# Strassen steps' first sums: transfers bound to leave one raw load sooner, four places for them instead of two, and steps of seven units in other places

## The chip, the cores and the metric

One core of one Trainium2 chip. The metric is the device time of one execution in microseconds. The kernel before took 2371.19 us, the median of three runs (2370.3 to 2372.21).

Names used below: PE is TensorE, DVE is VectorE, ACT is ScalarE, POOL is GpSimd, SP is SyncE. SP and POOL only issue DMA transfers here, apart from a few masks on POOL. Each engine works through its own list of instructions in order, so an instruction that waits holds up everything behind it on that engine.

## The reference

A decoder block on 256 tokens of width 4096, in float32:

```
h    = rmsnorm(x)
proj = h @ w_in                       # 4096 x 20480
u_p, z_p, u_c, b_c, c_c, z_c, g = split(proj)     # 6 x 2048, then 2 x 4096
y_pool = (causal pooling of u_p, then 4 maps 512x512) * pool_scale * silu(z_p)
y_conv = b_c * conv3(c_c * u_c) * silu(z_c)
br     = y_pool @ w_branch[0], y_conv @ w_branch[1]
merged = sum over both of sigmoid(g + gate_b) * br
out    = rmsnorm(x + merged @ w_out)
```

Nearly all arithmetic is the three products with w_in, w_branch and w_out. The inputs have 256 rows, so 128 partitions hold half of the tokens.

## The kernel before

**Units and steps.** The output columns are cut into 32 units of 1024 columns (the list `units`): twelve of the two mixers (cu0, cc0, cz0, cb0, cu1, cc1, cz1, cb1, pz0, pu0, pz1, pu1), eight gates (g0_0, g1_0, g0_1 ... g1_3), eight branch units (b0_0 ... b1_3) and four output units (o0 ... o3). A unit is a sum over 16 steps (8 in the branch units); a step multiplies 256 input channels, as stationary operands in the buffer `arena`, with one block of weights of 256 x 1024, which is 1 MB. The weights come once from memory, so each step needs one load of its block into one of three buffers of `raw` (NRAW = 3), issued by SP. The block is split into a high and a low part in fp32r (rounded by ACT, the rest subtracted by DVE), kept in a ring buffer (`ring`), and each product is three matmuls: high by high, high by low, low by high.

**P steps and S steps.** A plain step (P) makes 24 matmuls of 128x128 by 128x512; ACT and DVE make one pair of instructions for each half of the block. A Strassen step (S) makes 7 products instead of 8, so 21 matmuls, but its weights must be combined first. In `Step.micros` (kind "S") that is, on DVE: `sums` (V = first quarter of the block + two others), a subtraction for the three direct quarters, two additions into W, and one subtraction each for V's and W's low part; on ACT three roundings. S steps thus spare PE three matmuls and cost DVE several instructions. `PLACES` and `OUT` say which of a unit's 16 places hold S steps; for pz1 and g0_0 only how many there are counts, since `insert` weaves steps of the pooling branch ("B", "M") into these two units and orders the rest itself: P P B P M M P P, then the S steps in equal groups with one P between.

**Helped steps.** For the S steps that `HELPED` lists (by their number within the unit) the first sum need not be made on DVE. SP copies the first quarter of the block twice into a half of the buffer E (128 x 1024), POOL then adds the two other quarters to it with an accumulating DMA (`move_add`), and `sums` falls away; the load into `raw` leaves the first quarter out (768 KB). The two halves of E are the slots 0 and 1 (`place_of_sum`). `pump` sends such a transfer out when all of these hold:

- the step's unit is the running one, and E is free of the unit's epilogue: `e_done` writes into `sums_from` from which tick on (a tick is six matmuls);
- a slot is free (the step that had it has made its parts, `summed`);
- the step's own raw load is among the next ones: its number is below the number of the next load to be issued, `state["nl"]`, plus LEAD = 3, and not below `state["nl"]` + LATEST with LATEST = 0.

If the last bound is missed, the step is dropped from the list and makes its sum on DVE. "k loads ahead" below means that the step's own raw load is number `state["nl"]` + k when the copy is issued. The accumulating DMA is put on POOL's list WAIT = 1 raw load later.

**The order of the program.** Everything is laid out by a planner in Python when the kernel is built. `pump` issues raw loads as soon as the raw buffer's step is read, prepares steps up to AHEAD = 3 ahead of the running one as far as the ring has room, and issues the transfers of helped steps; `tick` runs one item of `queue`, the epilogue of the unit before (joining the Strassen sums into R, transposes on PE, gates, stores), and one item of the fills of `arena` for the branch units (`pop_fill`). E and R are the epilogue's buffers: banks are evacuated into E at a unit's end, R collects the unit's result. `joins` writes R once all S steps of the unit are done. `conv_units`, `pool_units`, `mix`, `gate_unit` and `out_unit` hold the epilogues with their stores of R (`z_d`, `gates_d`, `o_d`, by POOL).

Of the kernel before, what the change touches and what calls it, by code (L numbers as in the profile page):

```python
# [56 lines left out]
def hybrid_block(ctx: ExitStack, tc: tile.TileContext, x, x_t, norm_t, w_first, w_in, pool_w, pool_scale,  # L57
# [50 lines left out]
    R = sb("R", [P, 2, NU])  # L108
    E = sb("E", [P, 2, NU])
# [360 lines left out]
    def halves(fn):  # L470
        return [lambda t=t: fn(t) for t in range(2)]

    sums_from = [None]

    def e_done(n=2):

        def f():
            sums_from[0] = now[0] + n
        return f

    def combine(u):
# [67 lines left out]
    def gap(n):  # L549
        return [None] * n  # L550
# [66 lines left out]
    def at_places(at):  # L617
# [3 lines left out]

    few = NS_X - NB
    LAST_FIRST = ('cc0',)
    HELPED = {'cc0': (1, 2, 4, 5), 'cz0': (1, 2, 5), 'cb0': (1, 2, 4, 5, 7, 8), 'cu1': (1, 2, 4, 5, 7, 8), 'cc1': (1, 2, 4, 7, 8), 'cz1': (1, 2, 4, 5, 7), 'cb1': (1, 2, 4, 5, 7, 8), 'pz0': (1, 4, 5, 7), 'pu0': (1, 2, 4, 5, 7), 'pz1': (1, 2, 4, 5, 6, 7, 8), 'pu1': (1, 2, 4, 5, 7), 'g0_0': (1, 2, 4, 5, 7), 'g1_3': (1, 2, 5), 'g1_0': (1, 2, 4, 5, 8), 'g0_1': (1, 2, 4, 5, 6, 7), 'g1_1': (1, 4, 5, 7, 8), 'g0_2': (1, 2, 3, 4, 5, 7, 8), 'g1_2': (1, 2, 4, 5, 7, 8), 'g0_3': (1, 2, 4, 5, 7, 8), 'o0': (1, 2, 4, 5), 'o1': (1, 2, 4, 5, 7), 'o2': (1, 2, 4, 5), 'o3': (0, 2, 4, 5)}
    PLACES = {
# [19 lines left out]
    }  # L645
    GATE = (2, 4, 5, 7, 8, 10, 11, 13, 15)

# [149 lines left out]
    def mix(st):  # L797
        g = st.g
        for t in range(2):
            o = shared(2 * g + t)  # L800
            ts = slice(t * P, (t + 1) * P)
            for k in range(4):
                for i, (a, b) in enumerate(((st.ah, st.h), (st.ah, st.l), (st.al, st.h))):
                    pin(nc.tensor.matmul(o, a[:, k, ts], b[:, k], start=(k, i) == (0, 0), stop=(k, i) == (3, 2)))  # L804
        rg.release(st.bw, 16)
        rg.release(st.ba, 8)
        cs = slice(g * NH, (g + 1) * NH)
        for t in range(2):
            mul(R[:, t, cs], shared(2 * g + t), Y[:, t, cs])
        if g == 1:  # L810
            c = st.c

            def copy(j):
                act(chan(E)[:, 2 * j:2 * j + 2], bankview(j))
            queue.extend(gap(3) + transposes(R, copy) + [lambda: put(y_d[0, c], chan(E)), e_done(8)])


    def gate_unit(n, c, before=None):
# [214 lines left out]
    last = units[-1]  # L1033
# [175 lines left out]

    x_with = {0: (1, 2), 1: (2, 4), 3: (4, 6), 4: (6, 8), 5: (8, 10), 6: (10, 12)}  # L1210

    LATEST = 0
    LEAD, WAIT = 3, 1
    adding = deque()

    def pump():

        while True:
            moved = False
            nl = state["nl"]  # L1220
            if nl < len(loaded) and (nl < NRAW or loaded[nl - NRAW].split):
                issue_load(loaded[nl])
                state["nl"] += 1

                if nl in x_with:
                    load_x(*x_with[nl])
                moved = True
            while helped and (helped[0].prepared or helped[0].load_index < state["nl"] + LATEST):
                helped.pop(0)
            if helped and helped[0].host is running[0] and sums_from[0] is not None and now[0] >= sums_from[0] and (  # L1230
                    helped[0].load_index < state["nl"] + LEAD):
                t = helped[0]
                at = next((i for i in t.slots if sums_in[i] is None or sums_in[i].summed), None)
                if at is not None:
                    helped.pop(0)
                    t.slot, sums_in[at] = at, t
                    w, v = t.src.rearrange("p k n -> p (k n)"), place_of_sum(at)
                    load(v, w[:, None, 0:NH].to_broadcast([P, 2, NH]))
                    adding.append((state["nl"] + WAIT, t, v, w[:, NH:3 * NH]))
                    moved = True  # L1240
            while adding and (adding[0][0] <= state["nl"] or adding[0][1].load_index < state["nl"]):
                _, t, v, w = adding.popleft()
                move_add(v.rearrange("p i n -> p (i n)"), w)
                t.added = True
                moved = True
            i = state["np"]
            if i < len(steps) and i <= state["limit"]:
                s = steps[i]
                if s.src is None or s.raw is not None:
                    if state["micros"] is None:  # L1250
                        state["micros"] = deque(s.micros())
                    if state["micros"]:
                        size, guard, fn = state["micros"][0]
                        if guard is None or guard():
                            block = rg.alloc(size) if size else True
                            if block is not None:
                                state["micros"].popleft()
                                fn(block)
                                moved = True
                    if not state["micros"]:  # L1260
                        s.prepared = s.split = True
                        state["micros"] = None
                        state["np"] += 1
                        moved = True
            if not moved:
                return
# [5 lines left out]
    for u in units:  # L1272
        for k, s in enumerate(t for t in u.steps if t.kind == "S"):
            if k in HELPED.get(u.name, ()):
                helped.append(s)
        s_at = [i for i, t in enumerate(u.steps) if t.kind == "P"]
        for i, t in enumerate(u.steps):
            t.slots = (0, 1)[:1 + (i < s_at[-1])] if t.kind == "S" else ()
    sums_in = [None] * 2
    running = [None]  # L1280

    def tick():
# [91 lines left out]
    for u in units:  # L1374
        if u.name == "pu1":
            make_bands(1)
            u.steps[2].first.append(lambda: end_bands(1))
        if u is last_x:
            Y = replace_by("y_b", lower).tile([P, 2, NU], F32, name="Y")
            stages.append(replace_by("more").tile([P, 4, P], F32, name="sb"))  # L1380

            in_y = [Y.rearrange("p a n -> p (a n)")[:, i * 4 * P:(i + 1) * 4 * P].rearrange("p (k c) -> p k c", k=4) for i in range(2)]
            stages.extend(in_y)
        if u is last:
            break
        sums_from[0] = None
        if u is units[1]:
            e_done()()
        for st in u.steps:
            assert st.prepared, (u.name, st.kind)  # L1390
            if st is u.steps[0]:
                running[0] = u
            if st is u.steps[-1]:
                running[0] = None
                assert all(t is None or t.summed for t in sums_in)
            run_step(u, st)
            state["now"] += 1
            if u is last_x and st is u.steps[12]:
                units_done[0] = True
            if u.s and not u.flags.get("joined") and st is not u.steps[-1] and u.closed(*SHARED):  # L1400
                assert not queue, u.name
                queue.extend(joins(u))
            pump()
            if u is units[units.index(last_x) - 1] and st is u.steps[14]:
                queue_fills()
            if u.before and st is u.steps[len(u.steps) * 3 // 4]:
                assert not queue, u.name
                if u.name == "b0_0":
                    del stages[2:]
                    assert not any(f.st is q for f in fills for q in in_y)  # L1410
                u.before()
        while queue:
            f = queue.popleft()
            if f:
                f()
        combine(u)
        queue.extend(u.epi(u))
        state["mm"] = 0
        pump()

# [6 lines left out]
        parked[c] = raw[:, i % NRAW].rearrange("p (t n) -> p t n", t=2)  # L1427
        load(parked[c], o_d[c])

    sums_from[0], running[0] = None, last  # L1430
    lead = last.steps[:-TAIL]
    combined = False
    for st in lead:
# [153 lines left out]
```

## Time and profile before

| what | value |
|---|---|
| median of three runs | 2371.19 us |
| the profiled execution | 2372.17 us |
| its span in the profile | 2370.1 us |
| matmuls | 10474 |
| PE busy | 2351.0 us, 99% |
| DVE busy | 2187.4 us, 92% |
| ACT busy | 1422.8 us, 60% |
| moved by DMA | 590.92 MB, 249 GB/s |
| TensorE clock granted | 0.999 of full |

The profiled execution's time is 2.07 us above its span, what lies before the first and behind the last instruction. The profile lists groups of instructions by line and tile, waits (which engine stood idle, and what ended that), stretches of time with each engine's busy share, and each engine's instructions in order of time. The start of a unit is the start of its first matmul.

### The profile page before, as it was taken

The numbers are of one execution on the slowest core, as the hardware profiler recorded it, in microseconds if no ns is written. First come the engines' busy times: TensorE is split into PE (matmuls) and PEld (weight loads), VectorE is DVE, ScalarE is ACT, GpSimd is POOL, SyncE is SP. The second block draws the span as 40 slices with busy tenths as digits, with TensorE's granted clock in tenths as the row PEclk, the third lists the DMA queues.
The fourth block names the chain that finished last, engine by engine and source line by source line (L and its number), as shares of the span: only waits on it lengthen the run. The fifth ranks groups of instructions, "written<-read, shape, count | busy, mean of one in ns | idle before, by whom it ended". The sixth has DMA issues, their size and how long they took to land.

```text
span 2370.1 us, 28071 instructions
## 1 busy us (share of the span) xinstructions
PE 2351.0 (99%) x10474; PEld 1944.1 (82%) x10474; DVE 2187.4 (92%) x2247; ACT 1422.8 (60%) x1477; POOL 133.3 (6%) x200
## 2 busy tenths in 40 slices
PE   9999999999999999999999999999999999999998
PEld 7888888887888888888888888888788888888886
DVE  8999999989999989989989999998998898899898
ACT  7565665666556666566656656565664556566564
POOL 0000000000001001000000000001100001000000
PEclk9999999999999999999999999999999999999999
DMA  8576777766877657757887887788866667778767
GB/s 336 184 243 206 248 261 244 254 222 215 272 269 233 227 205 246 235 215 249 275 265 244 284 269 239 253 287 282 280 239 236 238 236 284 241 232 287 237 236 268
DMA packets 104841, 590.92 MB, mean 249 GB/s; under 512 B 11200, under 2 KB 11456, under 8 KB 50176
## 3 DMA queue, kind: packets, MB, share of 16 engines
q1 hardware_dynamic: 82944, 498.14, 57.5%
q0 software_dynamic: 21328, 89.93, 16.1%
q8 instruction: 82, 1.34, 0.2%
q10 hardware_dynamic: 432, 1.07, 0.1%
q14 instruction: 55, 0.45, 0.0%
HBM read 556.58 MB, written 25.17 MB: 245 GB/s over the span
## 4 chain that ended last, share of the span: by engine, by line
PE 89%; DVE 6%; DMA 3%; ACT 1%; issue 1%; DVEq 0%; SPq 0%; ACTq 0%
PE sums L1294 66%; PE shared L1294 21%; DVE ring L72 3%; DMA raw<-in_w_out_dram 1%; ACT ring L69 1%; DVE W L72 1%; PE shared L804 1%; PE shared L528 1%; DMA sb<-y_d 1%; DVE V L72 1%; DVE R L72 1%; DMA E<-in_w_in_dram 0%; DMA raw<-in_w_first_dram 0%; DVE arena L72 0%; ACT E L69 0%
## 5 line engine op out<-in xcount | busy, mean ns | idle before, releaser
L1294 PE MATMUL sums<-ring,arena 128*128 128x512 f32 x7596 | 1797.9, 390 | 4.3 <-DVE ring L72 1.8
L1294 PEld LDWEIGHTS sums<-ring,arena 128*128 128x128 f32 x7596 | 1422.5, 188 | 302.1 <-DVE ring L72 2.8
L72 DVE TENSOR_TENSOR ring<-raw,ring 128x1024 fp32r<-128x1024 f32 (+2 forms) x692 | 940.1, 1385 | 88.8 <-ACT ring L69 85.3
L69 ACT ACTIVATE ring<-raw 128x1024 fp32r<-128x1024 f32 (+2 forms) x692 | 797.6, 1184 | 228.9 <-PE sums L1294 123.7
L1294 PE MATMUL shared<-ring,arena 128*128 128x512 f32 x2520 | 636.7, 389 | 2.4 <-DVE ring L72 2.4
L1294 PEld LDWEIGHTS shared<-ring,arena 128*128 128x128 f32 x2520 | 472.4, 188 | 102.1 <-DVE ring L72 4.2
L69 ACT ACTIVATE ring<-W 128x1024 fp32r<-128x1024 f32 x210 | 223.1, 1062 | 379.1 <-DVE W L72 319.6
L69 ACT ACTIVATE ring<-V 128x1024 fp32r<-128x1024 f32 x158 | 167.4, 1059 | 181.2 <-DVE V L72 153.2
L72 DVE TENSOR_TENSOR ring<-W,ring 128x1024 fp32r<-128x1024 f32 x210 | 257.4, 1226 | 17.8 <-ACT ring L69 5.6
L72 DVE TENSOR_TENSOR V<-raw 128x1024 f32<-128x1024 f32 x158 | 192.8, 1220 | 1.6 <-DMA raw<-in_w_in_dram 1.6
L72 DVE TENSOR_TENSOR ring<-V,ring 128x1024 fp32r<-128x1024 f32 x158 | 192.7, 1220 | 0.4 <-ACT ring L69 0.4
L72 DVE TENSOR_TENSOR W<-W,raw 128x512 f32<-128x512 f32 x210 | 144.0, 686 | 0.0
L72 DVE TENSOR_TENSOR W<-V,raw 128x512 f32<-128x512 f32 x158 | 109.3, 692 | 4.9
L94 POOL DMA_DIRECT2D E<-in_w_in_dram x47 | 41.1, 876 | 766.8 <-DMA E<-in_w_in_dram 373.7
L72 DVE TENSOR_TENSOR R<-R,E 128x1024 f32<-128x1024 f32 (+1 forms) x49 | 77.3, 1592 | 4.5 <-DMA R<-in_gate_b_dram 3.4
L72 DVE TENSOR_TENSOR ring<-E,ring 128x1024 fp32r<-128x1024 f32 x56 | 68.3, 1219 | 1.6 <-ACT ring L69 1.5
L69 ACT ACTIVATE ring<-E 128x1024 fp32r<-128x1024 f32 x56 | 58.7, 1048 | 17.0 <-DMA E<-in_w_in_dram 5.3
L72 DVE TENSOR_TENSOR R<-R,shared 128x512 f32<-128x512 f32 x87 | 59.6, 685 | 1.9
L72 DVE TENSOR_TENSOR W<-E,raw 128x512 f32<-128x512 f32 x52 | 36.0, 691 | 25.9 <-DMA E<-in_w_in_dram 14.7
L69 ACT ACTIVATE arena<-sa 128x512 fp32r<-128x512 f32 (+2 forms) x48 | 25.3, 556 | 54.6 <-DVE sa L72 50.3
L69 ACT ACTIVATE E<-sums,rin 128x512 f32<-128x512 f32 x76 | 49.3, 682 | 13.3 <-PE sums L1294 13.2
L72 DVE TENSOR_TENSOR arena<-sa,arena 128x512 fp32r<-128x512 f32 (+2 forms) x48 | 27.5, 599 | 3.8 <-ACT arena L69 3.8
(143 smaller groups left out, 557.0 us busy)
## 6 DMA issues: line engine op xcount, KB each, us to landing
raw<-in_w_in_dram SPq DMA_DIRECT2D x271, 1024.0 KB, 5.0
raw<-in_w_branch_dram SPq DMA_DIRECT2D x64, 1024.0 KB, 5.3
raw<-in_w_out_dram SPq DMA_DIRECT2D x59, 1024.0 KB, 5.0
raw<-in_w_in_dram SPq DMA_DIRECT2D x47, 768.0 KB, 6.2
E<-in_w_in_dram SPq DMA_DIRECT2D x47, 512.0 KB, 6.8
E<-in_w_in_dram POOLq DMA_DIRECT2D x47, 512.0 KB, 8.3
gates_d<-R POOLq DMA_DIRECT2D x8, 1024.0 KB, 11.4
R<-in_gate_b_dram POOLq DMA_DIRECT2D x7, 1024.0 KB, 13.6
```

Of the source, the lines that this page charges most:

```text
L69: return pin(nc.scalar.activation(dst, src, func, **kw))
L72: return pin(nc.vector.tensor_tensor(out=dst, in0=a, in1=b, op=op))
L94: return pin(nc.gpsimd.dma_start(dst, src, accum_op=ALU.add))
L528: pin(nc.tensor.transpose(shared(j)[:, i * T + t * P:i * T + (t + 1) * P], src[:, t, c:c + P], ident))
L804: pin(nc.tensor.matmul(o, a[:, k, ts], b[:, k], start=(k, i) == (0, 0), stop=(k, i) == (3, 2)))
L1294: pin(nc.tensor.matmul(ps, lhs, rhs, start=n == 0, stop=n == u.total[b] - 1))
```

## The change

1. **Four slots.** Slots 2 and 3 are the halves of R. `place_of_sum` already names them; `sums_in` has four entries, and a step tries 0, 2, 3, 1 in this order, slot 1 only when a P step still follows in the unit.
2. **Two times instead of one.** `sums_from` holds one for E and one for R. R is released by a new item `e_done(8, 1)` at the end of every epilogue but those of pu and b0 units, that is eight ticks after the last item (a store of R in most units); in the unit with the mixed pooling steps by `e_done(2, 1)` behind the transposes, and once at the start of the second unit.
3. **LATEST = 1, LEAD = 4.** A transfer goes out one to three raw loads ahead of the step's own, where it was zero to two. A step that can't is dropped from the list.
4. **Places.** Those of cz0, cu1, cz1, cb1, g0_0, g1_0 and g1_3 are changed: cb1 has 8 S steps instead of 9, g0_0 9 instead of 8, the other five as many as before.
5. **HELPED.** cb1 lists (1, 2, 4, 5) instead of (1, 2, 4, 5, 7, 8), pz1 (1, 4, 5, 6, 8) instead of (1, 2, 4, 5, 6, 7, 8), o0 (1, 2, 4, 5, 6) instead of (1, 2, 4, 5), o2 (0, 1, 2, 4, 5) instead of (1, 2, 4, 5).

```diff
-    sums_from = [None]
-    def e_done(n=2):
+    sums_from = [None, None]
+    def e_done(n=2, which=0):
         def f():
-            sums_from[0] = now[0] + n
+            sums_from[which] = now[0] + n
...
-        "cz0": (5, 7, 8, 9, 10, 11, 14, 15),
+        "cz0": (5, 7, 8, 9, 10, 12, 14, 15),
-        "cu1": (4, 5, 7, 8, 10, 11, 12, 13, 15),
+        "cu1": (5, 6, 7, 8, 10, 11, 12, 13, 15),
-        "cz1": (5, 6, 7, 8, 9, 10, 13, 14, 15),
-        "cb1": (2, 4, 5, 7, 8, 10, 12, 13, 14),
+        "cz1": (5, 6, 7, 9, 10, 11, 12, 14, 15),
+        "cb1": (2, 4, 8, 9, 10, 12, 14, 15),
-        "g0_0": (3, 6, 7, 8, 10, 12, 14, 15),
-        "g1_0": (2, 4, 5, 7, 8, 10, 12, 13, 15),
+        "g0_0": (3, 5, 6, 7, 8, 10, 12, 14, 15),
+        "g1_0": (2, 4, 5, 6, 8, 10, 12, 13, 15),
-        "g1_3": (3, 6, 7, 9, 11, 13, 14),
+        "g1_3": (3, 6, 7, 9, 10, 11, 14),
...
-            queue.extend(gap(3) + transposes(R, copy) + [lambda: put(y_d[0, c], chan(E)), e_done(8)])
+            queue.extend(gap(3) + transposes(R, copy) + [e_done(2, 1), lambda: put(y_d[0, c], chan(E)), e_done(8)])
...
-    LATEST = 0
-    LEAD, WAIT = 3, 1
+    LATEST = 1
+    LEAD, WAIT = 4, 1
...
-            if helped and helped[0].host is running[0] and sums_from[0] is not None and now[0] >= sums_from[0] and (
+            if helped and helped[0].host is running[0] and (
                     helped[0].load_index < state["nl"] + LEAD):
                 t = helped[0]
-                at = next((i for i in t.slots if sums_in[i] is None or sums_in[i].summed), None)
+                at = next((i for i in t.slots if sums_from[i // 2] is not None and now[0] >= sums_from[i // 2]
+                           and (sums_in[i] is None or sums_in[i].summed)), None)
...
-            t.slots = (0, 1)[:1 + (i < s_at[-1])] if t.kind == "S" else ()
-    sums_in = [None] * 2
+            t.slots = (0, 2, 3, 1)[:3 + (i < s_at[-1])] if t.kind == "S" else ()
+    sums_in = [None] * 4
...
-        sums_from[0] = None
+        sums_from[:] = [None, None]
         if u is units[1]:
             e_done()()
+            e_done(2, 1)()
...
         queue.extend(u.epi(u))
+        if u.name[:2] not in ('pu', 'b0'):
+            queue.append(e_done(8, 1))
```

More of the change, by code (lines that the diff above doesn't have):

```diff
@@ L623, in hybrid_block @@
     LAST_FIRST = ('cc0',)
-    HELPED = {'cc0': (1, 2, 4, 5), 'cz0': (1, 2, 5), 'cb0': (1, 2, 4, 5, 7, 8), 'cu1': (1, 2, 4, 5, 7, 8), 'cc1': (1, 2, 4, 7, 8), 'cz1': (1, 2, 4, 5, 7), 'cb1': (1, 2, 4, 5, 7, 8), 'pz0': (1, 4, 5, 7), 'pu0': (1, 2, 4, 5, 7), 'pz1': (1, 2, 4, 5, 6, 7, 8), 'pu1': (1, 2, 4, 5, 7), 'g0_0': (1, 2, 4, 5, 7), 'g1_3': (1, 2, 5), 'g1_0': (1, 2, 4, 5, 8), 'g0_1': (1, 2, 4, 5, 6, 7), 'g1_1': (1, 4, 5, 7, 8), 'g0_2': (1, 2, 3, 4, 5, 7, 8), 'g1_2': (1, 2, 4, 5, 7, 8), 'g0_3': (1, 2, 4, 5, 7, 8), 'o0': (1, 2, 4, 5), 'o1': (1, 2, 4, 5, 7), 'o2': (1, 2, 4, 5), 'o3': (0, 2, 4, 5)}
+    HELPED = {'cc0': (1, 2, 4, 5), 'cz0': (1, 2, 5), 'cb0': (1, 2, 4, 5, 7, 8), 'cu1': (1, 2, 4, 5, 7, 8), 'cc1': (1, 2, 4, 7, 8), 'cz1': (1, 2, 4, 5, 7), 'cb1': (1, 2, 4, 5), 'pz0': (1, 4, 5, 7), 'pu0': (1, 2, 4, 5, 7), 'pz1': (1, 4, 5, 6, 8), 'pu1': (1, 2, 4, 5, 7), 'g0_0': (1, 2, 4, 5, 7), 'g1_3': (1, 2, 5), 'g1_0': (1, 2, 4, 5, 8), 'g0_1': (1, 2, 4, 5, 6, 7), 'g1_1': (1, 4, 5, 7, 8), 'g0_2': (1, 2, 3, 4, 5, 7, 8), 'g1_2': (1, 2, 4, 5, 7, 8), 'g0_3': (1, 2, 4, 5, 7, 8), 'o0': (1, 2, 4, 5, 6), 'o1': (1, 2, 4, 5, 7), 'o2': (0, 1, 2, 4, 5), 'o3': (0, 2, 4, 5)}
     PLACES = {
         "cc0": (2, 4, 6, 7, 10, 12, 15),
[1 row of a table removed]
[1 row of a table added]
         "cb0": (2, 4, 5, 7, 8, 10, 12, 14, 15),
[1 row of a table removed]
[1 row of a table added]
         "cc1": (2, 4, 5, 7, 8, 10, 12, 13, 15),
[2 rows of a table removed]
[2 rows of a table added]
         "pz0": (4, 5, 6, 8, 10, 11, 13, 14, 15),
@@ L1428, in unpark @@
         load(parked[c], o_d[c])
-    sums_from[0], running[0] = None, last
+    sums_from[:], running[0] = [None, None], last
     lead = last.steps[:-TAIL]
```

## The prediction

> **What bounds the kernel now.** I read the page's busy lines first, then the stretches of single units, then who waited for whom.
>
> ```profile
> span 2370.1 us, 28071 instructions
> ...
> PE 2351.0 (99%) x10474; PEld 1944.1 (82%) x10474; DVE 2187.4 (92%) x2247; ACT 1422.8 (60%) x1477; POOL 133.3 (6%) x200
> ```
>
> PE is busy 99% of the span, and DVE 92%: two engines close to full. The reader is to see how little can be won without taking matmuls away. What a matmul costs shows in a stretch with nothing else:
>
> ```profile
> 1195.10 21.92 PE L1294 MATMUL sums<-ring,arena 128*128 128x512 f32 x96
> ```
>
> 96 matmuls in 21.92 us, the last with its own 0.39 us, is 0.227 us from start to start. A P step (24) then takes PE 5.44 us, an S step (21) 4.76. Two stretches that each hold one unit of nine S and seven P steps (357 matmuls, 80.9 us) show where more time goes:
>
> ```profile
> core 0: us, PE busy (x) PEld busy (x) DVE busy (x) ACT busy (x) POOL busy (x), PEclk, DMA share, GB/s
> ...
> 1114.20:1195.10 80.90, 80.90 (x358) 66.99 (x357) 75.72 (x72) 50.04 (x49) 4.87 (x6) 1.00 0.79 257
> 1195.10:1278.00 82.90, 81.39 (x358) 66.85 (x357) 75.37 (x72) 48.63 (x48) 5.30 (x6) 1.00 0.83 260
> ```
>
> The first (g1_0) runs at exactly the matmuls' rate: PE never stands. The second (g0_1) has the same matmuls and takes 2.0 us more. The waits of PE's weight loads between 20 and 2350 us give the whole bill:
>
> ```profile
> PEld shared L1294 <- DVE ring L72: 4.2, 5, 1.9
> PEld sums L1294 <- DVE ring L72: 2.8, 3, 1.1
> PEld sums L1294 <- ACT E L69: 2.6, 3, 1.4
> PEld sums L1294 <- ACT ring L69: 1.0, 2, 0.8
> ```
>
> That is 10.6 us in 13 waits, 0.45% of the run. By unit (the same view on cz1, pz1, g0_1, g1_3, b0_0):
>
> ```profile
> PEld sums L1294 <- DVE ring L72: 1.7, 2, 1.1
> PEld shared L1294 <- DVE ring L72: 1.0, 2, 0.8
> PEld sums L1294 <- ACT ring L69: 0.8, 1, 0.8
> PEld sums L1294 <- DVE ring L72: 1.1, 1, 1.1
> PEld sums L1294 <- ACT ring L69: 0.2, 1, 0.2
> PEld shared L1294 <- DVE ring L72: 2.3, 2, 1.9
> PEld shared L1294 <- DVE ring L72: 0.9, 1, 0.9
> PEld sums L1294 <- ACT E L69: 1.1, 2, 0.8
> ```
>
> cz1 3.5, pz1 1.3, g0_1 2.3, g1_3 0.9, b0_0 1.1; the other 1.5 of "ACT E" stand at b0_0's end. In g0_1 2.3 us of such waits are 2.0 us of time (above), so I count 0.87 of each. No other unit stalls.
>
> Why DVE is late there:
>
> ```profile
> DVE W L72 <- DMA E<-in_w_in_dram: 14.7, 7, 5.0
> ...
> DVE W L72 <- DMA E<-in_w_out_dram: 5.2, 1, 5.2
> ```
>
> ```profile
> 575.23 0.69 DVE L72 TENSOR_TENSOR W<-E,raw 128x512 f32<-128x512 f32 x1 [2.61 <-DMA E<-in_w_in_dram]
> 925.72 0.69 DVE L72 TENSOR_TENSOR W<-E,raw 128x512 f32<-128x512 f32 x1 [0.77 <-DMA E<-in_w_in_dram]
> 1227.21 0.69 DVE L72 TENSOR_TENSOR W<-E,raw 128x512 f32<-128x512 f32 x1 [3.40 <-DMA E<-in_w_in_dram]
> 1634.66 0.69 DVE L72 TENSOR_TENSOR W<-E,raw 128x512 f32<-128x512 f32 x1 [4.99 <-DMA E<-in_w_in_dram]
> ```
>
> DVE stood 19.9 us, eight times, for a helped sum that had not landed. Four of these waits, 11.8 us together, are shown from the order of time: they lie in cz1, pz1, g0_1 and g1_3, the four units in which PE then waits for DVE. The 5.2 is in o2, where DVE was far enough ahead; three short ones share the other 2.9 us.
>
> **The change, part by part.** *Matmuls: nothing.* cb1 gives up an S step (+3 matmuls), g0_0 gains one (-3); the other five units only move theirs. So all of the result is stalls, and no more than 10.6 x 0.87 = 9.2 us can go.
>
> *Going out one load sooner (LATEST).* A transfer has two legs:
>
> ```profile
> raw<-in_w_in_dram SPq DMA_DIRECT2D x271, 1024.0 KB, 5.0
> ...
> E<-in_w_in_dram SPq DMA_DIRECT2D x47, 512.0 KB, 6.8
> E<-in_w_in_dram POOLq DMA_DIRECT2D x47, 512.0 KB, 8.3
> gates_d<-R POOLq DMA_DIRECT2D x8, 1024.0 KB, 11.4
> ```
>
> One behind the other is 15.1 us. A load is issued three steps before its block is split, three steps at 4.76 to 5.44 are 14.3 to 16.3 us: a copy that goes out just before its own raw load (0 ahead) is as likely late as not. One load more adds about 5 us. I walked the planner's rules through the program before: of 52 helped steps 18 go out 0 ahead. The four waits shown and the 5.2 of o2 are all among these 18. Of the three short ones two are 1 ahead, and there PE did not stall. So at least 11.8 + 5.2 = 17.0 of DVE's 19.9 us should go; up to 2.9 stay.
>
> *How many stay helped.* With LATEST = 1 a slot can serve again only five steps later, and a step that finds none returns to DVE. Walked by hand: lost are one each in cc0, cz1, pu1, cb1, g0_1, g1_3 and o2; R's halves, open from about tick 27 (step 7) on, win the step at place 15 of cb0, cc1, g1_1, g0_2, g1_2 and g0_3, one more in cu1, two in pz1. That is some 54 against 52. What a sum on DVE costs, and the steps around it:
>
> ```profile
> 549.43 1.22 DVE L72 TENSOR_TENSOR V<-raw 128x1024 f32<-128x1024 f32 x1
> ...
> 556.12 0.69 DVE L72 TENSOR_TENSOR W<-E,raw 128x512 f32<-128x512 f32 x1
> ...
> 561.43 4.63 DVE L72 TENSOR_TENSOR ring<-raw,ring 128x1024 fp32r<-128x1024 f32 x4
> ```
>
> A plain S step takes DVE 556.12 - 549.43 = 6.7 us, a helped one 561.43 - 556.12 = 5.3, a P step 4.63 / 2 = 2.3. Against PE's own step a plain S loses 1.9 us of lead, a helped one 0.5, and a P wins 3.1, as far as the ring has room. Two more helped steps are worth 2.8 us of DVE in a whole run: nothing by themselves. The number hardly moves; the times of departure do.
>
> *Unit by unit.* g0_1: the helped step 7, late by 3.40, becomes a plain one for 1.4, so DVE is 2.0 ahead of before there, and 9 and 10 are helped: all 2.3 goes. pz1: four helped steps instead of two, no late one: 1.3 goes. g1_3: the helped step 7 (4.99 late) turns plain, a gain of 3.6 in front of the fills: 0.9 goes, and with it the front of b0_0 (1.1), where ACT was late with banks for the same reason. cz1: before, six S steps stand in a row (5 to 10) and PE first waits at the fifth. Now step 6 is plain (-1.4), a P at 8 takes a plain S step's place (3.1 + 1.9 = +5.0), so DVE comes to step 9 about 3.6 ahead; a helped step and two plain ones cost 0.5 + 1.9 + 1.9 = 4.3, so 0.7 to 0.8 of stall stays ahead of the P at 13, and the late step 14 goes out two ahead. Of 3.5 go 2.7. The 1.5 at b0_0's end is ACT behind a fill, which nothing here touches. Sum: 2.7 + 2.3 + 1.3 + 0.9 + 1.1 = 8.3, times 0.87: 7.2 us.
>
> *What the places cost.* pu1 loses its help at place 12, but starts with more lead from pz1: I put 0.4. g0_0 takes the pattern of pz1 (three S, P, three S, P, three S) with three helped steps: by pz1 no stall without a late transfer. cb1 gets three P steps behind place 4 and is easier than before; cu1 has four S steps in a row from 5, right behind five P steps, where the lead is at the ring's limit. Together 0.4 for these. cz0 and g1_0: nothing seen.
>
> *R as a slot.* No transfer of before goes to R, so its wait is not in the trace. SP must wait until the store of R has read it:
>
> ```profile
> 1221.96 0.57 POOL L91 DMA_DIRECT2D gates_d<-R  x1 [2.29 <-ACT R L69]
> ```
>
> ```profile
> 1231.33 0.38 SPq L87 DMA_DIRECT2D E<-in_w_in_dram  x1
> ```
>
> In g0_1 the store lands at 1221.96 + 11.4 (last row of the legs above) = 1233.4. The copy that the planner put at tick 20 (1195.1 + 20 x 1.36 = 1222.3) really left at 1231.3, 9 us behind; one at tick 27 would leave near 1241. Margin: 7 to 8 us. So I take nothing; the ends are 0 and, if SP reached R at tick 27 exactly (1231.8), 1.6 us per unit of SP's time, which delays the raw loads behind it: two steps, 9.5 us and more, less the 5.0 that they take to land leave those 4.5 to spare. The copy's 512 KB also share the DMA engines with raw loads, but the number of copies stays.
>
> **Sum:** 7.2 - 0.4 - 0.4 = 6.4 us. The profiled execution took 2372.17 (span 2370.1), so 2365.8; the median of the runs lies 1.0 below it: 2364.8 against 2371.19, 0.27% faster.
>
> **The rivals.** *New stalls eat the gain.* Plain steps where helped ones stood (cz1, pu1, o0, o2), four S steps in a row in cu1: each plain step more costs 1.4 of lead, and where it is gone, that is time. With 2 us in cz1, 1 in pu1 and 1 in cu1 the gain is 3.2: 2368.0. For it: DVE is 92% busy. Against: in the units named a P step or more lead stands in front.
>
> *The sums come late all the same.* If the second leg is held up on POOL, an earlier first leg helps nothing; then DVE's 19.9 us stay, about 1 us comes from the places: 2370.
>
> ```profile
> L94 POOL DMA_DIRECT2D E<-in_w_in_dram x47: 851/860/1018, 104.8 to 1645.5; - x47
> ```
>
> (Shortest, median and longest issue in ns.) For it: POOL works in order, so whatever waits there holds up the second legs behind it. Against it: an issue takes 851 to 1018 ns, whatever DVE does, and first legs that land sooner let POOL go on sooner. The Trainium skill has a rule for this side: in "SBUF - State Buffer", section "SBUF: two separate sides", it says that a transfer issued from GpSimd gets no descriptors while DVE holds the shared port in a two-port operation. By that rule the second leg would be late however early the first is, and the time would stay near 2370. The trace disagrees as far as it goes: with DVE at 92% the longest of 47 issues is 1.02 us.
>
> *Slower: SP waits for R.* One mechanism: a copy into R stands in SP's order ahead of raw loads; if R's store lands later than the margin of 7 to 8 us allows, all raw loads behind are late, in g0_1, g1_1, g0_2, g1_2 and g0_3, where a store of R of 11.4 us precedes it. Raw loads have 4.5 us to spare, so it decides from about 12 us of delay; at 2.5 us of stall in each of five units, +12.5 - 6.4, it gives 2377. Against it: no store of before is that late, and these units run at 80.9 now.
>
> **How the numbers follow.** Forecast (a gain of 4.8 to 9) 0.55; new stalls 0.22; late all the same 0.13; SP waits for R 0.10. About 0.2%, 4.7 us, is what a measurement of this kernel can tell from no change: the forecast lies beyond it, the next two within. So faster 0.55, same 0.34, slower 0.11. The range runs from 2362.0, where every stall is gone (9.2), up through the new stalls and most of the late case to 2370.5; what is left out is the slower rival and the rest of the late case, about 0.18.
>
> **What would show it.** Right: DVE's waits for E fall from 19.9 to under 5 us; g0_1's stretch is 80.9 to 81.2 long, pz1's about 1 and cz1's about 2.3 shorter than before; PEld's waits sum to 2 to 4 us; raw loads land in about 5.0 us as before. Wrong: waits of DVE for R or E by whole us; SP waiting for a DMA that reads R; new PEld waits in cu1, pu1 or cz1; or a gate unit longer than 81 us.

## The result, and the profile after

| | median, us | runs |
|---|---|---|
| before | 2370.45 | 20 runs, 2367.5 to 2374.5 |
| after | 2366.43 | 20 runs, 2362.4 to 2369.3 |

The ratio is 0.9982, with a 95% interval of 0.9975 to 0.9989: 2.6 to 5.9 us faster, about 4.3. The forecast was 6.4. The two profiled executions took 2372.17 and 2366.17 us, 6.0 apart, which is more than the medians differ, since the first lies 1.7 above its median. 5.3 of these 6.0 us are gone when the last matmul starts; the other 0.7 lies behind it, and nothing in the change explains it.

The page after, its busy times. The reader is to see that nothing was taken from any engine: the same 10474 matmuls, the same 2247 instructions on DVE.

```profile
span 2364.1 us, 28084 instructions
...
PE 2349.5 (99%) x10474; PEld 1944.1 (82%) x10474; DVE 2187.1 (93%) x2247; ACT 1421.3 (60%) x1477; POOL 133.6 (6%) x200
```

The time is in a few units. The stretches of single units, before (cz1, pz1, g0_0, g1_3, b0_0; g0_1 stands in the prediction), then after (cz1, pz1, g0_0, g0_1, g1_3, b0_0). The first two numbers of a row are its bounds, rounded to 0.1 us, the third its length; the engines' columns are in the order of the prediction's table.

```profile
504.70:590.60 85.90, 84.18 (x374) 68.26 (x373) 81.87 (x87) 50.27 (x53) 3.44 (x4) 1.00 0.72 221
...
835.90:934.50 98.60, 97.84 (x455) 81.24 (x455) 86.73 (x80) 59.30 (x59) 11.91 (x16) 1.00 0.63 210
1016.10:1114.20 98.10, 98.10 (x458) 81.84 (x457) 83.44 (x78) 60.81 (x59) 4.20 (x5) 1.00 0.68 232
...
1601.70:1684.90 83.20, 82.70 (x364) 67.86 (x362) 74.75 (x82) 48.95 (x53) 9.53 (x15) 1.00 0.81 276
1684.90:1729.10 44.20, 42.85 (x187) 34.75 (x186) 38.24 (x51) 28.45 (x36) 4.53 (x7) 1.00 0.82 282
```

```profile
504.50:587.60 83.10, 83.10 (x374) 68.45 (x373) 81.84 (x87) 49.16 (x52) 2.58 (x3) 1.00 0.67 216
...
833.70:931.10 97.40, 97.40 (x455) 81.26 (x454) 86.29 (x80) 59.34 (x59) 13.34 (x17) 1.00 0.65 220
1012.70:1110.10 97.40, 97.40 (x454) 81.27 (x453) 86.52 (x81) 59.29 (x59) 3.34 (x4) 1.00 0.63 213
1191.00:1271.90 80.90, 80.90 (x358) 67.00 (x357) 77.90 (x74) 50.95 (x49) 4.39 (x5) 1.00 0.82 271
1595.60:1680.70 85.10, 83.49 (x365) 67.84 (x364) 76.75 (x84) 49.33 (x53) 8.64 (x14) 1.00 0.76 262
1680.70:1723.80 43.10, 42.62 (x188) 34.65 (x186) 36.81 (x49) 28.06 (x35) 4.52 (x7) 1.00 0.83 290
```

cz1 gives 2.8 us, pz1 1.2, g0_1 2.0, b0_0 1.1; g0_0's 0.7 for its additional S step goes back to cb1, which has one less. g1_3 *costs* 1.9: its 363 matmuls need 82.3 us, and it takes 85.1. 2.8 + 1.2 + 2.0 + 1.1 - 1.9 = 5.2, all of what is gone at the last matmul but a tenth.

DVE's waits after, and four neighbouring groups of its transfers' list (the last number is the median from issue to landing, in us):

```profile
DVE sa L72 <- DMA sa<-y_d: 3.6, 1, 3.6
...
DVE W L72 <- DMA E<-in_w_in_dram: 1.6, 1, 1.6
```

```profile
E<-in_w_in_dram SPq DMA_DIRECT2D x33, 512.0 KB, 6.6
E<-in_w_in_dram POOLq DMA_DIRECT2D x33, 512.0 KB, 9.4
gates_d<-R POOLq DMA_DIRECT2D x8, 1024.0 KB, 12.4
R<-in_w_in_dram SPq DMA_DIRECT2D x15, 512.0 KB, 7.1
```

The waits for late sums fell from 19.9 us to 1.6, and the number of helped steps did not rise: 33 in E and 15 in R, with four more from w_out that is 52, as before. The largest wait of DVE for a transfer that was not there before is 3.6 us, for a fetch of a fill (sa). It lies in g1_3.

### The profile page after: what moved, and what is told of

Same layout as the page of the kernel before. It is cut to its first block, busy times and chain, and to the rows that moved or that the text cites. A ratio compares the mean times of both kernels' runs of the same rounds, so it can differ in the third digit from the quotient of the medians.

```text
span 2364.1 us, 28084 instructions
## 1 busy us (share of the span) xinstructions
PE 2349.5 (99%) x10474; PEld 1944.1 (82%) x10474; DVE 2187.1 (93%) x2247; ACT 1421.3 (60%) x1477; POOL 133.6 (6%) x200
## 4 chain that ended last, share of the span: by engine, by line
PE 97%; DVE 1%; DMA 0%; ACT 0%; issue 0%; SPq 0%; DVEq 0%; ACTq 0%
PE sums L1295 71%; PE shared L1295 24%; PE shared L804 1%; DVE ring L72 1%; PE shared L528 1%; DMA raw<-in_w_branch_dram 0%; ACT ring L69 0%; DVE W L72 0%; DMA raw<-in_w_first_dram 0%; DVE arena L72 0%; PE shared L783 0%; DVE V L72 0%; DVE sa L72 0%; PE shared L784 0%; PE shared L786 0%
## 5 line engine op out<-in xcount | busy, mean ns | idle before, releaser
L72 DVE TENSOR_TENSOR ring<-raw,ring 128x1024 fp32r<-128x1024 f32 (+3 forms) x692 | 940.3, 1385 | 93.1 <-ACT ring L69 90.4
L69 ACT ACTIVATE ring<-raw 128x1024 fp32r<-128x1024 f32 (+3 forms) x692 | 797.1, 1184 | 230.3 <-PE sums L1295 126.9
L94 POOL DMA_DIRECT2D E<-in_w_in_dram x33 | 28.7, 870 | 583.4 <-DMA E<-in_w_in_dram 355.8
L72 DVE TENSOR_TENSOR ring<-E,ring 128x1024 fp32r<-128x1024 f32 x40 | 48.8, 1221 | 1.5 <-ACT ring L69 1.5
L69 ACT ACTIVATE ring<-E 128x1024 fp32r<-128x1024 f32 x40 | 41.8, 1045 | 5.4 <-PE sums L1295 2.2
L72 DVE TENSOR_TENSOR W<-E,raw 128x512 f32<-128x512 f32 x36 | 24.8, 689 | 3.6 <-DMA E<-in_w_in_dram 1.6
```

Of the source, the lines that this page charges most:

```text
L69: return pin(nc.scalar.activation(dst, src, func, **kw))
L72: return pin(nc.vector.tensor_tensor(out=dst, in0=a, in1=b, op=op))
L94: return pin(nc.gpsimd.dma_start(dst, src, accum_op=ALU.add))
```

## The experiments

**Which part makes the gain.** My theory was that it is the departure one load sooner; the rival, the slots and the places. Four kernels take the change apart.

*Leaving sooner alone:*

```diff
 (before)
-    LATEST = 0
-    LEAD, WAIT = 3, 1
+    LATEST = 1
+    LEAD, WAIT = 4, 1
```

> The kernel before with LATEST = 1 and LEAD = 4 alone: two slots, old places, old lists. My theory, that the gain is the waits for late sums: DVE's waits for E fall from 19.9 to under 4 us; g0_1's stall of 2.0, most of g1_3's 0.9 and b0_0's first one go; cz1 keeps 1 to 2 of its 2.9 (fewer helped steps), pz1 keeps its 1.1; total 3 to 5 us under before, 2366 to 2367. Rival (places and the two new slots make the gain, since fewer steps find a slot): within 1.5 us of before, the stalls of g0_1 and g1_3 gone but new ones where steps lost their help.

2366.52 us against 2370.96 (ratio 0.9981, 0.9973 to 0.9990): as much as the whole change, with only 39 helped steps instead of 52. DVE's waits for E are 1.9 us. g0_1, g1_3 and b0_0 have no stall left (80.9, 82.3 and 42.2 us); cz1 keeps about 1.3 (84.1), and pz1 is half a microsecond longer (99.1), with one helped step where it had two. So 13 sums more on DVE cost less than the late ones did. And "sooner" is only a part of it: of the five late steps that the prediction names, one is still helped in the trace of this run, step 14 of cz1, and now in time. The other four (step 7 of g0_1 and of g1_3, the last S step of pz1, step 11 of o2) found no place before the new bound and make their sums on DVE. So here the bound works mostly by dropping the steps that would be late. A kernel with just these four taken out of the lists was not run.

*Places and lists alone* (the kernel before with all lines of PLACES and HELPED of the diff, LATEST = 0, two slots):

> The kernel before with the places and the lists of helped steps of after, but LATEST = 0, LEAD = 3 and two slots as before. My theory (late sums make the stalls): g0_1 keeps its 2.0 us of stall and DVE its waits for E of 12 us or more; cz1 gains about 1 to 2 by its P at 8; g1_3 with three S steps in a row and late sums stalls 2 to 4; total within 2 us of before, 2369 to 2372. Rival (the places make the gain): 3 us or more under before, under 2368.

2372.44 against 2371.79 (ratio 1.0002, 0.9993 to 1.0011): nothing. What cz1 wins (84.0 instead of 85.9) g1_3 loses (86.4 instead of 83.2), and the waits for late sums are all there:

```profile
DVE W L72 <- DMA E<-in_w_in_dram: 13.4, 5, 6.5
DVE W L72 <- DMA E<-in_w_out_dram: 4.7, 1, 4.7
```

*Everything but leaving sooner:*

```diff
 (after)
-    LATEST = 1
-    LEAD, WAIT = 4, 1
+    LATEST = 0
+    LEAD, WAIT = 3, 1
```

> The kernel after with LATEST = 0 and LEAD = 3 again, its four slots and places kept: transfers may again leave just before their own raw load. My theory: late sums return (DVE's waits for E from 1.6 to over 8 us), g0_1 stalls 1 to 2 us again and cz1 1 to 2, total 2 to 4 us more than the kernel after, 2368.5 to 2370.5. Rival (the slots and places carry the gain): within 1 us of the kernel after, 2365.5 to 2367.5.

2370.77 against 2371.79 (ratio 0.9994, 0.9985 to 1.0003): no gain, with 62 helped steps, the most of all. My sizes were off: g0_1 does not stall (80.9), cz1 does by 3.5 (86.3), and g1_3 takes 86.1. Late sums stand in both, 4.4 us of DVE's waits each:

```profile
DVE W L72 <- DMA E<-in_w_in_dram: 13.1, 5, 4.4
DVE W L72 <- DMA E<-in_w_out_dram: 4.4, 1, 4.4
```

39 helped steps, one of them late by 1.9 us, give 4.4 us; 62, of which six are late, give none that can be told.

*Everything but R:*

```diff
 (after)
-            t.slots = (0, 2, 3, 1)[:3 + (i < s_at[-1])] if t.kind == "S" else ()
+            t.slots = (0, 1)[:1 + (i < s_at[-1])] if t.kind == "S" else ()
```

> The kernel after with the slots 2 and 3 (halves of R) never offered: two slots in E as before, the rest as after. Some 16 steps lose their help. My theory (R's halves matter little, times of departure do): only pz1 and cu1 run short of lead there (pz1 stalls 0.5 to 1.5, cu1 up to 0.5), total 0.5 to 2 us more than the kernel after, 2367 to 2368.5. Rival (without R's halves the later departure bound would cost what it wins): 4 us more, as before, 2370.

2367.80 (ratio to before 0.9990, 0.9981 to 0.9999), again with 39 helped steps. pz1 is 99.0 us (1.6 more than after) and g0_0 98.4 (1.0 more, which I had not expected); cu1, which I had, stays. In the two units that carry the mixed pooling steps R's halves are worth 2.6 us, and pz0 is 0.5 longer without them (83.4); g1_3 and b0_0 are 2.9 shorter together. The profiled execution, with 2366.0 the fastest of the eleven, shows no loss as a whole, and the two intervals to before overlap: whether R's halves gain anything in all stays open.

**What stands behind g1_3's stall.** The branch units' operands are filled there: POOL fetches them into sa, sb and Y, ACT and DVE split them into `arena`. POOL, then DVE, then PE in the kernel after:

```profile
1625.31 0.89 POOL L94 DMA_DIRECT2D E<-in_w_in_dram  x1 [12.95 <-DMA E<-in_w_in_dram]
1625.88 0.88 POOL L91 DMA_DIRECT2D sa<-y_d  x1
1626.42 0.87 POOL L91 DMA_DIRECT2D gates_d<-R  x1
```

```profile
1636.52 1.02 DVE L72 TENSOR_TENSOR sa<-sa 128x128 f32<-128x128 f32 x4 [3.64 <-DMA sa<-y_d]
```

```profile
1653.69 0.73 PE L1295 MATMUL shared<-ring,arena 128*128 128x512 f32 x2 [0.99 <-DVE ring L72]
...
1659.64 10.99 PE L1295 MATMUL sums<-ring,arena 128*128 128x512 f32 x47 [0.50 <-DVE ring L72]
```

The landing of that one fetch, from the view of sa over 1624 to 1640 us, and of the store of R, from that of gates_d:

```profile
DMA to landing us min/median/max: 10.6/10.6/10.6
```

```profile
DMA to landing us min/median/max: 14.5/14.5/14.5
```

POOL issues the second leg of the helped step 11, and right behind it the fetch into sa. The fetch lands 10.6 us later, the store 14.5, DVE stands 3.64 us for it, and the lead that is lost there is missing at the three S steps 9, 10 and 11. Theory A: the second leg in front of the fetch makes the stall. Theory B: three S steps in a row beside the fills are too many in any case.

```diff
 (after: e2)
-    HELPED = {... 'g1_3': (1, 2, 5), ...}
+    HELPED = {... 'g1_3': (), ...}
```

> The kernel after, with no helped step in g1_3 (its list in HELPED empty), so that no second leg stands on POOL ahead of the fills' fetches there; step 11 makes its sum on DVE, 1.4 us more. Theory A (POOL's order makes the stall): DVE's wait for sa falls from 3.6 us to under 1, g1_3's stall from 2.6 to under 0.6 in spite of the plain sum, total about 2 us less than the kernel after, 2364.4. Theory B (three S steps in a row): the wait may go, but the stall stays at 2 to 4 us, total 2366 to 2368.

2364.20 (ratio to before 0.9970, 0.9959 to 0.9982). In the profiled execution (2362.89, the fastest of six) g1_3 takes 82.4 us with the same three S steps in a row and one plain sum more. POOL's row of that fetch, and when it landed:

```profile
1623.90 0.54 POOL L91 DMA_DIRECT2D sa<-y_d  x1 [11.12 <-DVE arena L72]
```

```profile
DMA to landing us min/median/max: 4.2/4.2/4.3
```

4.2 to 4.3 us (two fetches in this stretch) where it was 10.6, and DVE does not wait. That is A's number, and B falls. The fetch also leaves sooner. In both kernels DVE has read sa for the last time at 1623.6 us; here POOL issues the fetch 0.3 us later, in the kernel after only at 1625.88, since POOL stood with the second leg in front until the first had landed (the 12.95 us above). So about 2.0 us of the delay are POOL's waiting, and 6.3 the slower landing. The other way round:

```diff
 (after: e1)
-        "g1_3": (3, 6, 7, 9, 10, 11, 14),
+        "g1_3": (3, 6, 7, 9, 11, 13, 14),
```

> The kernel after, with the S steps of g1_3 at their places of before (3, 6, 7, 9, 11, 13, 14) instead of (3, 6, 7, 9, 10, 11, 14); all else as after. After the change g1_3's stretch is 85.05 us long where the matmuls need 82.3, so 2.6 us of stall. Theory A (POOL's order): the fetch of a fill (sa<-y_d) stands on POOL behind the second leg of a helped step, DVE waits 3.6 us for it, and that takes DVE's lead: the helped step is now number 13 instead of 11, its legs go out later, so the wait moves or shrinks, and 0.3 to 1.2 us of stall are left. Theory B (three S steps in a row are too many beside the fills, with or without that wait): the stall goes to 0 to 0.3 although DVE still waits about 3 us for sa. Both: 2365 to 2364 where the kernel after takes 2366.4 and before 2370.5.

2362.29 (ratio to before 0.9963, 0.9951 to 0.9976): **the fastest version**, under both kernels. The helped step is now number 13, its copy leaves later, and the second leg comes behind the fetch in POOL's order; the fetch lands after 4.4 us, the leg after 11.0 (9.2 in the kernel after):

```profile
1625.02 0.54 POOL L91 DMA_DIRECT2D sa<-y_d  x1 [12.62 <-DVE arena L72]
1625.55 0.55 POOL L91 DMA_DIRECT2D gates_d<-R  x1
1626.08 0.55 POOL L91 DMA_DIRECT2D Y<-y_d  x1
1629.35 0.89 POOL L94 DMA_DIRECT2D E<-in_w_in_dram  x1 [2.72 <-DMA E<-in_w_in_dram]
```

```profile
1591.80:1674.10 82.30, 82.30 (x365) 68.13 (x363) 77.25 (x84) 51.78 (x56) 8.63 (x14) 1.00 0.79 272
```

82.3 us, the matmuls' own time, PE busy throughout. DVE has no wait for sa at all; I had put 0.3 to 1.2 us of stall for A, and this run alone would not have told A from B.

The same kernel as after gives the dose, since the landing differs from run to run:

> The kernel after, unchanged, for a second profile of g1_3. Theory A (a second leg that stands on POOL ahead of the fill's fetch makes the stall, as far as both legs land late): DVE's wait for sa and g1_3's stall change together from run to run, the stall about the wait less 1, between 0 and 5 us, and nothing else in the profile changes by more than 0.5 us. Theory B (the three S steps make it): g1_3's stall is 2.6 us again, within 0.3, whatever the wait.

> The kernel after, unchanged, for a third profile of g1_3; expected as for the second.

The second profile (2366.74 us), then the third (a single run of 2367.5): DVE's wait for sa, and g1_3's stretch.

```profile
DVE sa L72 <- DMA sa<-y_d: 4.4, 1, 4.4
```

```profile
1595.90:1681.70 85.80, 83.81 (x365) 67.79 (x364) 76.69 (x84) 49.15 (x53) 8.62 (x14) 1.00 0.76 258
```

```profile
DVE sa L72 <- DMA sa<-y_d: 3.4, 1, 3.4
```

```profile
1595.80:1680.60 84.80, 83.20 (x365) 67.82 (x364) 76.67 (x84) 48.99 (x52) 8.64 (x14) 1.00 0.78 258
```

| profile | DVE waits for sa | g1_3 over 82.3 us |
|---|---|---|
| after | 3.6 | 2.8 |
| after, second | 4.4 | 3.5 |
| after, third | 3.4 | 2.5 |
| without R | 0.9 | 0.55 |
| no help in g1_3 | 0 | 0.1 |
| places back | 0 | 0 |

Wait and stall go together, the stall a little under the wait in these profiles. The same fetch is late in the two kernels in which R opens sooner (below): waits of 4.0 and 4.3 us, stalls of 4.4 and 3.5. Where sums also come late in g1_3 (places and lists alone: 3.0 us; everything but leaving sooner: 4.4) the stall is 4.1 and 3.8 with waits for sa of only 2.3 and 1.0, so this fetch is one cause of a stall there and not the only one. The runs' spread fits: the kernel after ran from 2362.4 to 2369.3 us, the one with g1_3's places back only from 2362.0 to 2362.7; no run at either end of the wide spread was profiled. b0_0 takes 43.1, 42.7 and 44.5 us in the three profiles, so in the third it changed by more than the expected 0.5; with the places back it takes 42.2, its 186 matmuls' time.

> The kernel after with g1_3's places of before once more, beside the kernel after on the same chip. If what is left of g1_3's stall is what separates the two: 2362.3 again, 3 to 5 us under the kernel after, with its runs within 1 us of each other, and no stall in g1_3. If the first result was the chip's: nearer to the kernel after, 2364 to 2366.

On another occasion, beside the kernel after at 2367.13 (ratio of that one to before 0.9979, 0.9970 to 0.9988): 2362.52, ratio to before 0.9961 (0.9947 to 0.9974), five runs within 0.7 us. So the first result stands.

**Does SP wait for R?** This was the prediction's slower rival. The release of R was moved:

```diff
 (after)
-            queue.append(e_done(8, 1))
+            queue.append(e_done(0, 1))
```

and in a second kernel to `e_done(4, 1)`.

> The kernel after with R open as soon as the epilogue has issued its last item, e_done(0, 1) instead of e_done(8, 1): SP then may reach a copy into R before the store of R has read it. By the margin in the prediction (7 to 8 us, 8 ticks are 10.9 us) SP waits 3 to 4 us for the store in the gate units, and raw loads have 4.5 us to spare: SP's waits for a DMA that reads R appear, some 10 to 20 us in all, the gate units stay at 80.9 us, total within 1.5 us of the kernel after. Rival (a copy that waits on SP holds the raw loads and PE with them): gate units of 82 us or more, total 4 us or more above the kernel after, 2370.5.

2374.87 against 2371.79: slower than before (ratio 1.0017, 1.0008 to 1.0026). My expectation failed, the rival's came in: g1_1, g0_2, g1_2 and g0_3 take 82.2, 82.0, 83.7 and 83.0 us where they took 80.9, which is 7.2 us together. The chain shows in each: SP waits 6.8, 8.9, 10.8 and 8.9 us for the store, and DVE then 4.6, 3.2, 5.0 and 6.7 us for raw loads. In g0_1 SP waits 9.3 us too, DVE only 1.3, and 0.1 us is lost.

> The kernel after with R open four ticks after the epilogue instead of eight, e_done(4, 1): halfway to the run that opened it at once, took 2374.9 and had SP waiting 44.6 us for stores of gates (7.8 us in the kernel after). If these waits are the price, they lie between, 15 to 30 us, and the gate units' stalls too (together 1 to 4 us, 6.9 at once), total 2367 to 2371. If the price comes from something else that opening R brings (more copies, other steps helped): as at once, 2374, or as after, 2366.4.

2371.14 (ratio to before 0.9996, 0.9985 to 1.0006). SP's waits for the store of R, opened at once, after four ticks, after eight (the kernel after):

```profile
SPq L87 <- DMA gates_d<-R: 44.6, 5, 10.8
```

```profile
SPq L87 <- DMA gates_d<-R: 18.4, 5, 9.1
```

```profile
SPq L87 <- DMA gates_d<-R: 7.8, 4, 2.7
```

The dose is as expected: 44.6, 18.4 and 7.8 us of SP. With four ticks the profiled execution shows one gate unit late (g1_2, 82.1); but it took 2367.25, and the runs spread from 2365.4 to 2374.1, so what the slower ones lost is in no profile. More steps are helped from R as it opens sooner (16, 20 and 23), so these totals alone do not tell the waits from the copies; the chain in the units of the first run does. With eight ticks SP still waits up to 2.7 us, and no unit from g0_1 to g0_3 stalls. So the margin is used up: the copies no longer come after the store, and only the raw loads' slack hides it.

**More S steps?** With stalls gone, one S step more saves three matmuls, 0.68 us.

```diff
 (after, g1_3 as in e1: e8)
-        "cb1": (2, 4, 8, 9, 10, 12, 14, 15),
+        "cb1": (2, 4, 6, 8, 9, 10, 12, 14, 15),
...
-    OUT = (..., (2, 4, 5, 7, 8, 10, 11, 15), (2, 3, 4, 6, 10, 11, 13, 15), ...)
+    OUT = (..., (2, 4, 5, 7, 8, 10, 11, 13, 15), (2, 3, 4, 6, 8, 10, 11, 13, 15), ...)
```

> The kernel after with g1_3's places of before (as in the run that took 2362.3) and one S step more in each of three units whose lead was never under about 1.4 us in the profile after: cb1 (2, 4, 6, 8, 9, 10, 12, 14, 15), o1 (2, 4, 5, 7, 8, 10, 11, 13, 15), o2 (2, 3, 4, 6, 8, 10, 11, 13, 15), the lists of helped steps naming the same places as after. Nine matmuls fewer, 3 x 3 x 0.227 = 2.0 us. If the leads hold as reckoned (a plain S costs DVE 1.9 of lead, a P wins 3.1): 2360.3. Rival (DVE is full, and the next S step only moves the time into stalls): these units stall by 0.7 us or more each, total 2362 or above.

2365.27 (ratio to before 0.9974, 0.9965 to 0.9984): 3 us more than without these steps. cb1 and o1 give the 0.7 us of their three matmuls, and more is lost behind them: 0.6 in pz0, 0.3 in pu1, 1.4 in o3, and most in o2. The stretches of o1 and o2:

```profile
2104.20:2185.10 80.90, 80.90 (x358) 67.01 (x357) 77.35 (x73) 50.40 (x51) 5.40 (x7) 1.00 0.82 271
2185.10:2269.20 84.10, 81.93 (x359) 66.83 (x358) 81.33 (x78) 48.33 (x50) 2.35 (x3) 1.00 0.65 222
```

o1 takes its S step without a stall, but hands less lead on; o2, with DVE busy 81.33 of 84.10, is 3.1 us over its matmuls' 80.9. The leads of single units cannot be spent one by one.

## Why the prediction was right, and where it was wrong

**What bounds the kernel: right.** All of the change lies in PE's stalls, and these came from sums that landed late. Leaving sooner alone gives the gain, the rest without it gives none, and DVE's waits for E fell from 19.9 to 1.6 us (forecast: at most 2.9 left). What the forecast put down to going out one load sooner is, as the first experiment shows, mostly late steps returned to DVE, as it said itself of g0_1 and g1_3.

**Unit by unit.** In the profiles, against the forecast's 8.3 x 0.87:

| term | forecast, us | profile, us |
|---|---|---|
| cz1 | 2.3 | 2.8 |
| g0_1 | 2.0 | 2.0 |
| pz1 | 1.1 | 1.2 |
| b0_0 | 1.0 | 1.1 |
| g1_3 | 0.8 | -1.9 |
| pu1, cu1 and others (places) | -0.8 | 0 |

**Wrong: g1_3.** The step that failed reads "g1_3: the helped step 7 (4.99 late) turns plain, a gain of 3.6 in front of the fills: 0.9 goes". The late step 7 did go. But I looked only at the step that lost its help and not at the one that keeps it: the second leg of step 11 now stands on POOL just ahead of a fill's fetch, which I would have seen by walking POOL's order through that unit as I did SP's. The stall of 0.9 became one of 2.5 to 3.5, in three profiles, and the term came out 2.7 us worse than forecast. That the sum still came near (5.2 for 6.4) is in part luck: 0.8 put down for the places cost nothing, and cz1 gave 0.5 more. With g1_3 mended the time is 2362.3 to 2362.5, where the prediction set its floor at 2362.0 for "every stall is gone".

**Also off.** "The 1.5 at b0_0's end is ACT behind a fill, which nothing here touches": with g1_3's places back b0_0 runs at its matmuls' time, so that stall was handed on from g1_3. Of helped steps I counted 54, there are 52. In cz1 "0.7 to 0.8 of stall stays"; about 0.3 stayed, by the 82.87 us that cz1 takes when R opens at once. Of the signs that were set, PE's weight loads wait 4.9 us in all instead of 2 to 4 (3.2 of them in g1_3), and two signs of being wrong did appear: SP waits for a transfer that reads R, and g1_3 is a gate unit longer than 81 us, for the reason above.

**The rivals.** *The sums come late all the same* is out: second legs land in 9.4 us (median) instead of 8.3, and yet nearly all in time. The Trainium skill's rule about transfers issued from GpSimd ("SBUF — State Buffer", "SBUF: two separate sides") is about the time in which DVE holds the shared port in a two-port operation. No row here says that DVE's instructions are such, so the prediction's "the second leg would be late however early the first is" did not follow from it, and no run tests the rule. DVE is 93% busy, and the second legs into E are issued in 0.84 to 1.02 us each (minimum, median and maximum of 33 in the view of E on POOL after), and took 0.85 to 1.02 before:

```profile
L94 POOL DMA_DIRECT2D E<-in_w_in_dram x33: 842/856/1017, 112.0 to 1625.3; - x33
```

*SP waits for R* was right as a mechanism and wrong in its point. I had a margin of 7 to 8 us from one unit (g0_1), in which the store left POOL 19.7 ticks after the unit's start. In the kernel after, the stores in g0_1 and g0_2 land 13.8 and 14.7 us after their issue instead of the 11.4 reckoned with, the one in g1_2 leaves POOL 32.6 us after its unit's start (26.9 in the example), and SP waits 2.5, 2.7 and 2.4 us for these three. The margin was gone; what held was the slack of the raw loads, estimated there at 4.5 us. The chance of 0.10 for it was low for something that four ticks' difference brings near.

*New stalls eat the gain* came true in one place and for another reason than the S steps' cost: a transfer behind a transfer.

## What to carry to other kernels

Count what is late, not how much is offloaded: here 39 offloaded sums with one late ran 4.4 us faster than 52 with eight late, and 62 with six late no faster. When transfers are moved forward, walk every queue that they pass in order, here POOL's as well as SP's, and ask which transfer now stands behind which, since the next one late is often another stream's. And where runs of one kernel spread more than those of its neighbour, look for a wait that changes from profile to profile: it may be the one worth mending.

## What the runs showed of the hardware that I had not expected

A fetch of 256 KB issued by POOL right behind an accumulating transfer of 512 KB landed after 10.6, 11.5 and 11.1 us in three profiles of the kernel after, and after 7.8 to 11.2 in five other kernels with that order. In the six kernels without one just ahead, the one before among them, the same fetch took 4.3 to 7.2. The store of 1 MB that follows it landed after 11.2 to 14.7 us with the transfer in front and after 6.2 to 10.0 without. The Trainium skill, "DMA: Bandwidth & Descriptors", section "Issuing engines are not separate DMA queues", says that what is issued from any engine ends on the same DMA engines and interleaves. A fetch slowed by the transfer just ahead fits that; whether the two met on these engines or in POOL's queue no run here shows. What these runs add is that the order on POOL decides which comes late: with the fetch in front (g1_3's places back), the second leg landed after 11.0 and 10.8 us and the fetch behind it (sb) after 12.2 and 12.0. The fetch's issue itself was longer too right behind the accumulating transfer, 0.88 us instead of 0.54.
